# VectorE takes over the sums of squares and the sine products from GpSimd

## The chip, the cores and the metric

The kernel runs on one core of one Trainium2 chip, and all times are device microseconds (us) of that core. The core's engines run their own instruction streams and wait for each other through semaphores: TensorE (PE in the profile; PEld is its weight load), VectorE (DVE), ScalarE (ACT), GpSimd (POOL) and SyncE (SP), which starts the DMAs here.

## What is computed

Two networks run one after the other on 512 tokens of width 1024, all in float32. The first has two layers of this form:

```python
def hybrid_layer(x, ...):
    h = rms_norm(x, g_mix_pre)
    u = h @ w_in
    aq, ak, av, cu, rq, rk, rv, rg = jnp.split(u, SPLITS, axis=-1)
    y_att = chunk_attention(aq, ak, av, rel_bias)
    y_conv = conv_module(cu, conv_w, conv_b, conv_ln_g, conv_ln_b)
    y_ret = retention(rq, rk, rv, rg)
    mix = jnp.concatenate([y_att, y_conv, y_ret], axis=-1) @ w_out
    x = x + rms_norm(mix, g_mix_post)
    h = rms_norm(x, g_mlp_pre)
    f = jnp.square(jax.nn.relu(h @ w_up)) @ w_down
    return x + rms_norm(f, g_mlp_post)
```

`rms_norm` divides a row by the root of its mean square and multiplies by a gain. `retention` and one of the second network's attentions rotate queries and keys: `x1 * cos - x2 * sin`, `x2 * cos + x1 * sin`. The second network also has two layers, each a mixer of three attentions and a gated feed-forward (`silu(h @ w_gate) * (h @ w_up)) @ w_down`), with a plain residual after each.

## The kernel before

The activations stand with the 1024 features on partitions: eight tiles `x_1` to `x_8` (128 features by 512 tokens). Every product is made of three float32r matmuls. A weight chunk `raw` (128x1024) comes by DMA; ACT rounds it to `wh` (L511), DVE forms the rest `wl = raw - wh` (L513). A normalised input has `hh` from ACT (L682) and `hl` from DVE (L683). `dense` and `lin_tok` then issue `wh` by `hh`, `wh` by `hl` and `wl` by `hh` for each of the eight k (L529 to L531, and L546 to L548 in `lin_tok`), so one k needs all four.

A norm's factor is not applied to the input but to the product's output; it is made from a sum of squares over the features. `add_sq` squares a tile on ACT (`sq`, L677) and adds it to `acc` on POOL (L678). When all eight are in, PE sums over the partitions by a matmul with a column of ones (L663, into `po` or `pt`), DVE computes the inverse root in twelve small steps (`rstd`, L635 to L641) and spreads it (`bt`, L648), PE transposes that (L654) and ACT copies it to `rb` (L693), which every output of the product that follows is multiplied by.

Three places use it. `post_norm1` closes each half layer of the first network, in two halves of 256 tokens: after the half's factor, for each tile `f = f * gain * rb` (L1006), `x = x + f` (L1008), `hh`, `hl`, and the addition to `acc2`; of these additions the last tile's in the second half runs on DVE already (`DVE_ADDS = (7,)`), the others on POOL. `residual2` does the like in the second network for 512 tokens (L1025 for `x`), with one addition for each tile. The convolution's two channel halves are added once a layer (L887).

A rotation multiplies the tile by the cosine on DVE (L803), the tile with its halves swapped by DMA (`sw`) by the sine on POOL (L804, and L1400 in the second network), and adds the two on DVE (L805). L1386 multiplies the tables of cosine and sine by `rb` on POOL. POOL's other work is masks (L826, L1224) and memsets (L607, L1395).

The order of each engine's instructions is not the order of this code: the framework's scheduler replays the whole program with its own costs for each instruction and writes every engine's stream from that, so a change of an engine at some places moves rows on all engines. A weight's tile, `raw`, `wh` or `wl`, comes from a ring of buffers, and is reused when its last reader is done.

Of the kernel before, what the change touches and what calls it, by code (L numbers as in the profile page):

```python
# [15 lines left out]
ALU = mybir.AluOpType  # L16
# [45 lines left out]
HEAD_STEPS = 2  # L62
CHAIN = 2
FACTOR_LAG = 4
DVE_ADDS = (7,)

# [296 lines left out]
class Prog:  # L365
# [301 lines left out]
    def rms_bcast(self, accs, d, t0=0, t1=512, bank=None):  # L667
        return self.bcast_rows(self.mean_rstd(accs, d, t0, t1, bank), (t1 - t0) // 128, 1, bank)

    def add_sq(self, acc, x, first, eng=None):  # L670
        nc = self.nc
        if first:
            nc.scalar.activation(acc, x, AF.Square)
            return
        t = self.S(s="sq")
        w = t[:, :acc.shape[-1]]
        nc.scalar.activation(w, x, AF.Square)  # L677
        (eng or nc.gpsimd).tensor_tensor(acc, acc, w, op=ALU.add)  # L678

    def gained(self, x, g, hd, k, t0=0, t1=512):  # L680
        s, g = slice(t0, t1), g[:, k:k + 1]
# [100 lines left out]
    def mix1(self, l, hd, halves):  # L782
        nc, A = self.nc, self.A
# [10 lines left out]
        def rotated(nm, p):  # L794
            ps = opened.pop(nm) if p == 0 else self.lin(("w_in", nm, p), l, hd)
            j = 2 * (nm == "rk")
            raw, sw, ct, sn = self.scaled(ps, hd), self.S(s="sw"), self.S(s="ct"), self.S(s="sn")
            for a, b in ((0, 32), (32, 0), (64, 96), (96, 64)):
                nc.sync.dma_start(sw[a:a + 32], raw[b:b + 32])
            nc.sync.dma_start(ct, A["ret"][p, j])  # L800
            nc.sync.dma_start(sn, A["ret"][p, j + 1])
            yield
            nc.vector.tensor_tensor(raw, raw, ct, op=ALU.mult)  # L803
            nc.gpsimd.tensor_tensor(sw, sw, sn, op=ALU.mult)  # L804
            nc.vector.tensor_tensor(raw, raw, sw, op=ALU.add)  # L805
            if nm == "rq":
                rot["q", p] = self.movings(raw)
            else:
                rot["k", p] = [self.still(raw, i) for i in range(2)]
# [65 lines left out]
        def conv():  # L875
            cs = [self.S(s="cv") for _ in range(2)]
            for j in range(31):
                for p in range(2):
                    w, x = self.v("conv_w", l, 31 * p + j), cy[p][:, j:j + 512]
                    if j == 0:  # L880
                        nc.vector.tensor_scalar(cs[p], x, w, self.v("conv_b", l, p), op0=ALU.mult, op1=ALU.add)
                    else:
                        nc.vector.scalar_tensor_tensor(cs[p], x, w, cs[p], op0=ALU.mult, op1=ALU.add)
                if j % CONV_STEP == 0:
                    yield
            s = self.S(s="cs")
            nc.gpsimd.tensor_tensor(s, cs[0], cs[1], op=ALU.add)  # L887
            yield
            mu = self.ptr()
            mm(mu, self.m256, s, start=True, stop=True)  # L890
            acc = self.S(s="acc")
            for p in range(2):
                nc.vector.tensor_tensor(cs[p], cs[p], mu, op=ALU.subtract)
                self.add_sq(acc, cs[p], p == 0)
            yield
            rb = self.rms_bcast([acc], 256)
            z = []
            for p in range(2):
                z.append(self.S(s="z"))
                nc.vector.tensor_tensor(z[p], cs[p], rb, op=ALU.mult)  # L900
            yield
            for p in range(2):
                nc.scalar.activation(z[p], z[p], AF.Identity, scale=self.v("conv_ln_g", l, p),
                                     bias=self.v("conv_ln_b", l, p))
                t = self.S(s="th")
                nc.scalar.activation(t, z[p], AF.Tanh, scale=0.5)
                nc.vector.scalar_tensor_tensor(z[p], t, 1.0, z[p], op0=ALU.add, op1=ALU.mult)
            yield
            for p in range(2):
                mix[3 + p] = self.split(z[p], scale=0.5, s="mc")  # L910
# [36 lines left out]
        def out(o):  # L947
# [7 lines left out]
        opened = dict(zip(("rq", "rk"), self.open_mix((("w_in", "rv"), 384), [("w_in", "rq", 0), ("w_in", "rk", 0)],  # L955
                                                      l, hd, v_sink(rv), halves)))
        kinds = dict(rq=lambda p: rotated("rq", p), rk=lambda p: rotated("rk", p), cg=conv_gate, ca=conv_in,
                     ret=retention, conv=conv, rg=gate_ret, av=values, aq=att_q, ak=att_k, att=attention, wo=out)
        self.pipeline((job[0], kinds[job[0]](*job[1:])) for job in ORDER1)
        return mix, f  # L960
# [24 lines left out]
    def post_norm1(self, xs, f, g_post, g_next):  # L985

        nc = self.nc
        acc, last, acc2, hd = self.S(s="acc"), self.S(s="last"), self.S(s="acc2"), Normed(self)

        def sink(i, o, ps, t0, t1):  # L990
            s = slice(t0, t1)
            nc.vector.tensor_tensor(f[o][:, s], ps, f[o][:, s], op=ALU.add)
            if i < 7:
                self.add_sq(acc[:, s], f[o][:, s], i == 0)
            else:
                nc.scalar.activation(last[:, s], f[o][:, s], AF.Square)

        def done(t0, t1):
            s = slice(t0, t1)
            y = self.mean_rstd([acc, last], 1024, t0, t1)  # L1000
            yield
            yield
            rb = self.bcast_rows(y, (t1 - t0) // 128, 1)
            yield
            for o in range(8):
                nc.vector.scalar_tensor_tensor(f[o][:, s], f[o][:, s], g_post[:, o:o + 1], rb,  # L1006
                                               op0=ALU.mult, op1=ALU.mult)
                nc.vector.tensor_tensor(xs[o][:, s], xs[o][:, s], f[o][:, s], op=ALU.add)  # L1008
                self.gained(xs[o], g_next, hd, o, t0, t1)
                self.add_sq(acc2[:, s], xs[o][:, s], o == 0, nc.vector if t1 == 512 and o in DVE_ADDS else None)  # L1010
                if o % CHAIN == CHAIN - 1:
                    yield
            if t1 == 512:
                self.after = self.factor_parts(hd, [acc2], FACTOR_LAG)

        return sink, done, hd

    def residual2(self, xs, scale, g_next, final=False):
# [359 lines left out]
    def nsa_in(self, l, hd, nx, nm, p=None):  # L1378

        nc, A = self.nc, self.A  # L1380
        if not nx:
            nx["ct"], nx["sn"], nx["q"], nx["x"] = self.S(s="ct"), self.S(s="sn"), {}, {}
            nc.sync.dma_start(nx["ct"], A["rope"][0])
            nc.sync.dma_start(nx["sn"], A["rope"][1])
            for t in (nx["ct"], nx["sn"]):
                nc.gpsimd.tensor_tensor(t, t, hd.rb, op=ALU.mult)  # L1386
        ps = self.lin(("w_in_2", nm) + (() if p is None else (p,)), l, hd)
        if nm == "vc":
            raw = self.scaled(ps, hd)
            yield  # L1390
        else:
            raw = self.S(s="raw")
            self.copy("raw", raw, ps)
            sw = self.S(s="sw")
            nc.gpsimd.memset(sw, 0.0)  # L1395
            for a, b in ((0, 8), (8, 0), (64, 72), (72, 64)):
                nc.sync.dma_start(sw[a:a + 8], raw[b:b + 8])
            yield
            nc.vector.tensor_tensor(raw, raw, nx["ct"], op=ALU.mult)
            nc.gpsimd.tensor_tensor(sw, sw, nx["sn"], op=ALU.mult)  # L1400
            nc.vector.tensor_tensor(raw, raw, sw, op=ALU.add)
        if nm == "nq":
            for g in range(2):
                nx["q"][p, g] = self.still(raw, g, -0.125)
        elif nm in ("ks", "kw"):
            nx[nm == "kw"] = self.movings(raw)
        else:

            nat = self.split(raw, s="nat")
            o, _ = VEC["pos_" + nm[0], l]  # L1410
            pos = self.vec[:, o:o + 16]
            x = nx["x"][nm[0]] = self.pools["x"].tile([128, 2, 2, 512], F32R, tag="x", name=self.nm("xs"))
            for i in range(2):
                for g in range(2):
                    r = slice(64 * g, 64 * g + 64)
                    nc.sync.dma_start(x[0:64, i, g, 0:496].bitcast(F32), nat[i][r, 0:496].bitcast(F32))
                    nc.sync.dma_start(x[64:128, i, g, 0:496].bitcast(F32), nat[i][r, 16:512].bitcast(F32))
                    if i == 0:
                        self.hi(x[:, i, g, 496:512], pos)
                    else:  # L1420
                        self.lo(x[:, i, g, 496:512], pos, x[:, 0, g, 496:512])
# [191 lines left out]
```

## Time and profile before

| | us |
|---|---|
| time, median of 3 runs (lowest, highest) | 3353.74 (3351.65, 3353.86) |
| the profiled execution, its own time | 3348.55 |
| span of its trace, first to last instruction | 3346.80 |
| PE busy | 3261.0 (97%) |
| DVE busy | 1949.7 (58%), 3381 instructions |
| ACT busy | 1343.6 (40%) |
| POOL busy | 284.3 (8%), 341 instructions |
| mean granted TensorE clock | 0.992 of full speed |

The busy times are shares of the whole span, which has stages of quite different kinds: a mixer with small matmuls, softmaxes and rotations; a feed-forward of large matmuls; and short stretches between them in which the norm's chain on DVE must run before the next product can. TensorE's clock has two levels, 2.4 GHz (1.00 in the profile) and 1.2 GHz (0.50). 1.75 us of the execution's time lie outside the span.

### The profile page before, as it was taken

Reading aid. Unit: us, or ns where it says so; the run is one execution under the profiler, and the core shown is the slowest. Engines: PE = TensorE matmul, PEld = TensorE weight load, DVE = VectorE, ACT = ScalarE, POOL = GpSimd, SP = SyncE. Lnnn points to the kernel's source line nnn. Section 1 sums busy time; section 2 is a strip of 40 time slices with the busy share of each in tenths; the row PEclk is TensorE's granted clock in tenths of the full one; section 3 lists DMA queues with packets and bytes.
Section 4 is the critical chain, followed back from the end, with each engine's and each line's share of the span. In section 5 each row is a group of like instructions: output and inputs, shape, how many; then the busy total and the mean of one; then the engine's idle time right before and its main releaser. Section 6 shows DMA issues by size and latency. Waiting matters only on the chain. (4 is left out here: it accounts for less than half of the span.)

```text
span 3346.8 us, 41207 instructions
## 1 busy us (share of the span) xinstructions
PE 3261.0 (97%) x15956; PEld 2678.4 (80%) x15956; DVE 1949.7 (58%) x3381; ACT 1343.6 (40%) x2254; POOL 284.3 (8%) x341
## 2 busy tenths in 40 slices
PE   8999999899999999999999999999999999999998
PEld 7778888877888888888777678888888877778887
DVE  5977334789734456454678654545445478664454
ACT  4464323436533333222566722223222356642222
POOL 2111000221200020000210000001000120010001
PEclk9999999999999999999999999999999999999999
DMA  5212222332132222222323022222222323112222
GB/s 169 98 64 95 95 97 99 116 130 82 65 106 95 101 95 95 95 97 99 111 81 120 26 95 97 98 95 95 98 97 95 120 75 101 67 70 100 96 95 69
DMA packets 100868, 317.29 MB, mean 95 GB/s; under 512 B 12608, under 2 KB 18112, under 8 KB 100672
## 3 DMA queue, kind: packets, MB, share of 16 engines
q1 hardware_dynamic: 100672, 314.66, 27.5%
q8 instruction: 125, 2.05, 0.2%
q14 instruction: 71, 0.58, 0.1%
HBM read 298.75 MB, written 6.29 MB: 91 GB/s over the span
## 5 line engine op out<-in xcount | busy, mean ns | idle before, releaser
L511 ACT ACTIVATE wh<-raw 128x1024 fp32r<-128x1024 f32 (+2 forms) x546 | 567.5, 1041 | 1401.6 <-PE pd L530 582.4
L513 DVE TENSOR_TENSOR wl<-raw,wh 128x1024 fp32r<-128x1024 f32 (+2 forms) x546 | 666.3, 1222 | 435.3 <-ACT wh L511 433.7
L529 PE MATMUL pd<-hh,wh 128*128 128x512 f32 (+1 forms) x1328 | 508.8, 385 | 3.2 <-ACT wh L511 3.2
L530 PE MATMUL pd<-hl,wh 128*128 128x512 f32 (+1 forms) x1328 | 508.4, 383 | 3.6 <-DVE hl L683 3.1
L531 PE MATMUL pd<-hh,wl 128*128 128x512 f32 (+1 forms) x1328 | 507.1, 382 | 2.1 <-DVE wl L513 2.1
L678 POOL TENSOR_TENSOR acc<-acc,sq 128x256 f32<-128x256 f32 (+1 forms) x160 | 172.7, 1083 | 2151.0 <-ACT sq L677 2148.6
L529 PEld LDWEIGHTS pd<-hh,wh 128*128 128x128 f32 x1328 | 251.5, 190 | 51.8 <-issue 3.7
L530 PEld LDWEIGHTS pd<-hl,wh 128*128 128x128 f32 x1328 | 252.1, 190 | 50.8 <-DVE hl L683 5.4
L531 PEld LDWEIGHTS pd<-hh,wl 128*128 128x128 f32 x1328 | 252.0, 190 | 48.5 <-DVE wl L513 2.5
L530 PE MATMUL pt<-hl,wh 128*128 128x512 f32 x480 | 188.8, 394 | 8.2 <-DVE hl L683 8.2
L530 PE MATMUL ps<-hl,wh 128*128 128x512 f32 (+1 forms) x528 | 196.6, 372 | 0.0
L529 PE MATMUL ps<-hh,wh 128*128 128x512 f32 (+1 forms) x528 | 196.2, 372 | 0.0
L531 PE MATMUL ps<-hh,wl 128*128 128x512 f32 (+1 forms) x528 | 196.1, 372 | 0.0
L531 PE MATMUL pt<-hh,wl 128*128 128x512 f32 x480 | 188.2, 393 | 0.0
L529 PE MATMUL pt<-hh,wh 128*128 128x512 f32 x480 | 187.8, 393 | 0.0
L529 PE MATMUL pd<-ah,wh 128*128 128x512 f32 (+1 forms) x498 | 185.0, 372 | 0.0
L530 PE MATMUL pd<-al,wh 128*128 128x512 f32 (+1 forms) x498 | 184.8, 371 | 0.0
L531 PE MATMUL pd<-ah,wl 128*128 128x512 f32 (+1 forms) x498 | 184.8, 371 | 0.0
L587 ACT ACTIVATE ah<-sc 128x512 fp32r<-128x512 f32 x88 | 55.6, 632 | 184.0 <-DVE sc L1131 184.0
L529 PE MATMUL pt<-ah,wh 128*128 128x512 f32 (+1 forms) x332 | 123.5, 372 | 0.0
L530 PE MATMUL ps<-al,wh 128*128 128x512 f32 (+1 forms) x332 | 123.4, 372 | 0.0
L531 PE MATMUL ps<-ah,wl 128*128 128x512 f32 (+1 forms) x332 | 123.3, 371 | 0.0
(476 smaller groups left out, 6483.8 us busy)
## 6 DMA issues: line engine op xcount, KB each, us to landing
raw<-in_w SPq DMA_DIRECT2D x514, 512.0 KB
raw<-in_w SPq DMA_DIRECT2D x20, 384.0 KB
xd<-x SPq DMA_DIRECT2D x16, 256.0 KB
x<-xd SPq DMA_DIRECT2D x16, 256.0 KB
sw<-sc SPq DMA_DIRECT2D x48, 64.0 KB
ct<-in_ret SPq DMA_DIRECT2D x12, 256.0 KB
sn<-in_ret SPq DMA_DIRECT2D x12, 256.0 KB
mst<-in_bias SPq DMA_DIRECT2D x12, 256.0 KB
```

Source lines behind the costliest of these rows:

```text
L511: nc.scalar.activation(h[:, :n], raw[:, :n], AF.Copy)
L513: eng.tensor_tensor(lo[:, :n], raw[:, :n], h[:, :n].bitcast(F32), op=ALU.subtract)
L529: mm(ps, h, rh[j][:, t0:t1], start=first and j == 0, stop=False)
L530: mm(ps, h, rl[j][:, t0:t1], start=False, stop=False)
L531: mm(ps, lo, rh[j][:, t0:t1], start=False, stop=last and j == n - 1)
L587: self.nc.scalar.activation(dst, src, AF.Copy, scale=scale)
L678: (eng or nc.gpsimd).tensor_tensor(acc, acc, w, op=ALU.add)
```

## The change

Six places change. `add_sq` loses its argument for the engine, and its addition is always DVE's; the constant `DVE_ADDS` goes, so code lines behind it move up by one. The four other products and sums named above are DVE's as well.

```diff
-DVE_ADDS = (7,)
...
-    def add_sq(self, acc, x, first, eng=None):
+    def add_sq(self, acc, x, first):
...
-        (eng or nc.gpsimd).tensor_tensor(acc, acc, w, op=ALU.add)
+        nc.vector.tensor_tensor(acc, acc, w, op=ALU.add)
...
             nc.vector.tensor_tensor(raw, raw, ct, op=ALU.mult)
-            nc.gpsimd.tensor_tensor(sw, sw, sn, op=ALU.mult)
+            nc.vector.tensor_tensor(sw, sw, sn, op=ALU.mult)
...
-            nc.gpsimd.tensor_tensor(s, cs[0], cs[1], op=ALU.add)
+            nc.vector.tensor_tensor(s, cs[0], cs[1], op=ALU.add)
...
-                self.add_sq(acc2[:, s], xs[o][:, s], o == 0, nc.vector if t1 == 512 and o in DVE_ADDS else None)
+                self.add_sq(acc2[:, s], xs[o][:, s], o == 0)
...
             for t in (nx["ct"], nx["sn"]):
-                nc.gpsimd.tensor_tensor(t, t, hd.rb, op=ALU.mult)
+                nc.vector.tensor_tensor(t, t, hd.rb, op=ALU.mult)
...
             nc.vector.tensor_tensor(raw, raw, nx["ct"], op=ALU.mult)
-            nc.gpsimd.tensor_tensor(sw, sw, nx["sn"], op=ALU.mult)
+            nc.vector.tensor_tensor(sw, sw, nx["sn"], op=ALU.mult)
```

190 instructions leave POOL: 114 additions of 128x256 and 46 of 128x512 (L678), 24 sine products (L804, L1400), 4 products of tables (L1386), 2 sums of the convolution (L887).

The scheduler's new order is shown at three places; in these rows a tile's name ends in a running number, `x_125` is the eighth tile of the activations, and the column at the end is partitions by elements.

The first place is DVE between the first network's first feed-forward and its second mixer (634 to 650 us of the trace). Before, in the middle of the chain of the second half's last tiles:

```order
L1006 SCALAR_TENSOR_TENSOR f_3488<-f_3488,vec,pt_5388 128x256
L683 SCALAR_TENSOR_TENSOR hl_4885<-x_124,vec,hh_4877 128x256
L1008 TENSOR_TENSOR x_125<-x_125,f_3488 128x256
L513 TENSOR_TENSOR wl_5490<-raw_5487,wh_5489 128x768
L683 SCALAR_TENSOR_TENSOR hl_4886<-x_125,vec,hh_4878 128x256
L678 TENSOR_TENSOR acc_852_4870<-acc_852_4870,sq_5478 128x256
L513 TENSOR_TENSOR wl_5520<-raw_5517,wh_5519 128x768
L513 TENSOR_TENSOR wl_5552<-raw_5549,wh_5551 128x768
```

The changed kernel has the same two conversions, `wl_5490` and `wl_5520`, in front of the chain, which begins with `f_3209`:

```order
L512 TENSOR_TENSOR wl_5458<-raw_5455,wh_5457 128x1024
L639 SCALAR_TENSOR_TENSOR a_5355<-a_5355,v_5353 128x2
L512 TENSOR_TENSOR wl_5490<-raw_5487,wh_5489 128x768
L640 SCALAR_TENSOR_TENSOR y_5354<-a_5355,y_5354 128x2
L647 COPY bt_5386<-y_5354 128x256
L512 TENSOR_TENSOR wl_5520<-raw_5517,wh_5519 128x768
L1005 SCALAR_TENSOR_TENSOR f_3209<-f_3209,vec,pt_5388 128x256
```

Both conversions have moved from the end of a chain of some 32 instructions to its start.

The second place is DVE between the second network's first mixer and its feed-forward (1922 to 1932 us). Before:

```order
L1025 SCALAR_TENSOR_TENSOR x_15167<-ps_16274,x_15167 128x512
L683 SCALAR_TENSOR_TENSOR hl_16114<-x_15163,vec,hh_16106 128x512
L513 TENSOR_TENSOR wl_16334<-raw_16331,wh_16333 128x1024
L513 TENSOR_TENSOR wl_16365<-raw_16362,wh_16364 128x1024
L683 SCALAR_TENSOR_TENSOR hl_16115<-x_15165,vec,hh_16107 128x512
L683 SCALAR_TENSOR_TENSOR hl_16116<-x_15167,vec,hh_16108 128x512
L635 TENSOR_SCALAR v_16298<-po_16293 128x4
```

The changed kernel, from the same `hl_16114` on:

```order
L682 SCALAR_TENSOR_TENSOR hl_16114<-x_15163,vec,hh_16106 128x512
L512 TENSOR_TENSOR wl_16253<-raw_16250,wh_16252 128x1024
L677 TENSOR_TENSOR acc_16100<-acc_16100,sq_16246 128x512
L1024 SCALAR_TENSOR_TENSOR x_15165<-ps_16249,x_15165 128x512
L1024 SCALAR_TENSOR_TENSOR x_15167<-ps_16274,x_15167 128x512
L512 TENSOR_TENSOR wl_16334<-raw_16331,wh_16333 128x1024
L682 SCALAR_TENSOR_TENSOR hl_16115<-x_15165,vec,hh_16107 128x512
L677 TENSOR_TENSOR acc_16100<-acc_16100,sq_16271 128x512
L682 SCALAR_TENSOR_TENSOR hl_16116<-x_15167,vec,hh_16108 128x512
L677 TENSOR_TENSOR acc_16100<-acc_16100,sq_16290 128x512
L512 TENSOR_TENSOR wl_16365<-raw_16362,wh_16364 128x1024
```

One of the two conversions that stood ahead of `hl_16115` and `hl_16116` now stands behind them; another, `wl_16253`, has come in from further ahead.

The third place is PE in the first network's first feed-forward (283 to 286 us), around the sum over the partitions of `acc2` (`po_2845`), whose second pair of matmuls waits for the second half's last addition. Before, that pair stands among the sixth tile's matmuls (`hh_2196`):

```order
L529 MATMUL ps_2584<-hh_2196,wh_2588 128x256
L530 MATMUL ps_2584<-hl_2204,wh_2588 128x256
L663 MATMUL po_2845<-ones_89,acc_421_2190 128x1 x2
L531 MATMUL ps_2584<-hh_2196,wl_2589 128x256
L529 MATMUL ps_2585<-hh_2196,wh_2638 128x256
```

The changed kernel has it between the seventh tile's (`hh_2197`) and the last one's (`hh_2198`):

```order
L529 MATMUL ps_2585<-hl_2205,wh_2638 128x256
L530 MATMUL ps_2585<-hh_2197,wl_2639 128x256
L662 MATMUL po_2845<-ones_89,acc_421_2190 128x1 x2
L528 MATMUL pd_2582<-hh_2198,wh_2290 128x256
L529 MATMUL pd_2582<-hl_2206,wh_2290 128x256
```

Sixteen matmuls of 128x256 have come in front of the pair.

## Rows read from the trace of the kernel before

**Rows 1.** The page: busy us (share of the span) and instructions of each engine.

```profile
PE 3261.0 (97%) x15956; PEld 2678.4 (80%) x15956; DVE 1949.7 (58%) x3381; ACT 1343.6 (40%) x2254; POOL 284.3 (8%) x341
```

**Rows 2.** Waits of PE: line, waited for whom; us in total, times, longest us.

```profile
PE pt L530 <- DVE hl L683: 8.2, 2, 4.1
PE ps L548 <- DVE wl L513: 7.9, 4, 6.8
...
PE po L663 <- DVE acc L678: 5.0, 3, 1.7
```

**Rows 3.** Lines of POOL by shape: names, shapes, count | busy us, mean ns | idle before.

```profile
L678 POOL TENSOR_TENSOR acc<-acc,sq 128x256 f32<-128x256 f32 x114 | 98.8, 871 | 853.6 <-ACT sq L677 852.1
L678 POOL TENSOR_TENSOR acc<-acc,sq 128x512 f32<-128x512 f32 x46 | 73.9, 1607 | 1297.4 <-ACT sq L677 1296.5
...
L804 POOL TENSOR_TENSOR sw<-sw,sn 128x512 f32<-128x512 f32 x12 | 17.3, 1441 | 91.7 <-DMA sn<-in_ret 64.1 <-DVE wl L513 26.6 <-PE pd L531 1.0
```

**Rows 4.** Lines of DVE by shape, the same columns.

```profile
L513 DVE TENSOR_TENSOR wl<-raw,wh 128x1024 fp32r<-128x1024 f32 x514 | 639.0, 1244 | 430.6 <-ACT wh L511 429.4
...
L683 DVE SCALAR_TENSOR_TENSOR hl<-x,vec,hh 128x512 fp32r<-128x512 f32 x48 | 46.6, 977 | 18.1 <-ACT hh L682 18.1
L1008 DVE TENSOR_TENSOR x<-x,f 128x256 f32<-128x256 f32 x64 | 41.3, 662 | 0.0
L683 DVE SCALAR_TENSOR_TENSOR hl<-x,vec,hh 128x256 fp32r<-128x256 f32 x64 | 38.1, 595 | 1.8 <-ACT hh L682 1.7
...
L805 DVE TENSOR_TENSOR sc<-sc,sw 128x512 f32<-128x512 f32 x12 | 8.2, 684 | 3.8 <-POOL sw L804 3.5
```

**Rows 5.** Timeline of DVE, 634 to 650 us: start us, duration us, instruction [idle before].

```profile
634.70 1.22 DVE L513 TENSOR_TENSOR wl<-raw,wh 128x1024 fp32r<-128x1024 f32 x1
...
638.08 0.42 DVE L1008 TENSOR_TENSOR x<-x,f 128x256 f32<-128x256 f32 x1
638.42 0.48 DVE L683 SCALAR_TENSOR_TENSOR hl<-x,vec,hh 128x256 fp32r<-128x256 f32 x1
638.81 0.48 DVE L1006 SCALAR_TENSOR_TENSOR f<-f,vec,pt 128x256 f32<-128x256 f32 x1
...
646.95 0.94 DVE L513 TENSOR_TENSOR wl<-raw,wh 128x768 fp32r<-128x768 f32 x1
...
648.22 0.41 DVE L678 TENSOR_TENSOR acc<-acc,sq 128x256 f32<-128x256 f32 x1
```

**Rows 6.** Timeline of PE, 640 to 658 us.

```profile
647.95 0.69 PE L548 MATMUL ps<-wl,hh 128*128 128x384 f32 x1 [6.77 <-DVE wl L513]
...
657.70 0.28 PE L529 MATMUL pd<-hh,wh 128*128 128x256 f32 x1
```

**Rows 7.** Timeline of ACT, 648 to 652 us.

```profile
650.84 0.84 ACT L511 ACTIVATE wh<-raw 128x768 fp32r<-128x768 f32 x1 [2.96 <-DMA raw<-in_w]
```

**Rows 8.** Timeline of DVE, 1924 to 1934 us.

```profile
1925.24 4.52 DVE L513 TENSOR_TENSOR wl<-raw,wh 128x1024 fp32r<-128x1024 f32 x2
1929.68 2.41 DVE L683 SCALAR_TENSOR_TENSOR hl<-x,vec,hh 128x512 fp32r<-128x512 f32 x2
```

**Rows 9.** Timeline of PE, 1926 to 1936 us.

```profile
1931.48 0.79 PE L530 MATMUL pt<-hl,wh 128*128 128x512 f32 x1 [4.12 <-DVE hl L683]
```

**Rows 10.** Timeline of PE, 282 to 290 us.

```profile
285.27 0.61 PE L663 MATMUL po<-ones,acc 128*128 128x1 f32 x4 [1.66 <-DVE acc L678]
```

**Rows 11.** Stretches A:B: us, busy of PE, PEld, DVE, ACT, POOL; granted clock, DMA share, GB/s.

```profile
120.00:140.00 20.00, 20.00 (x116) 19.02 (x115) 19.86 (x33) 9.79 (x15) 3.13 (x6) 1.00 0.38 132
284.00:292.00 8.00, 6.73 (x39) 6.32 (x40) 4.55 (x18) 3.04 (x5) 0.00 (x0) 0.79 0.00 0
644.00:652.00 8.00, 4.05 (x14) 4.05 (x15) 6.65 (x11) 2.73 (x6) 1.93 (x3) 0.57 0.31 108
1928.00:1936.00 8.00, 4.52 (x17) 3.80 (x18) 4.36 (x5) 1.06 (x1) 2.80 (x2) 0.79 0.39 131
2968.00:2980.00 12.00, 8.94 (x26) 7.39 (x27) 7.18 (x18) 1.06 (x1) 2.38 (x2) 0.57 0.31 112
```

## The prediction

> **What bounds the kernel now.** I read the page first: PE is busy for 3261.0 of 3346.80 us, so the kernel runs at the pace of its matmuls, and DVE and POOL matter only where PE waits for them or loses its clock after such a wait [rows 1]. The waits of PE come second. Three lines stand out that hang on what the change touches: the lower half `hl` of a normalised tile, 8.2 us in two waits; the weight's rest `wl`, 7.9 us, nearly all in one; and the last addition to a sum of squares, 5.0 us in three [rows 2]. Then I read those places in the timelines and the clock of the stretches around them. Everything else in the change is judged by whether it lengthens or shortens these waits or makes new ones.
>
> **What the moved work costs on DVE.** POOL loses 98.8 + 73.9 us for 160 additions and 17.3 us for 12 of the 30 products and sums [rows 3]; with the other 18 at the same 1.44 us that is 216 us, and POOL falls from 284 to about 68. On DVE an addition of 128x256 lasts 0.41 us, and its like, L1008, is followed by the next instruction after 0.34 us [rows 5]; a 128x512 addition lasts 0.68 us (L805) [rows 4]. So DVE gains 114 x 0.34 + 76 x 0.68 = 91 us.
>
> **What DVE gets back.** DVE's instructions that read two SBUF tiles are longer than their shortest in this trace. L1008 takes 0.42 us in the clear [rows 5] and 0.662 in the mean [rows 4]: 64 x 0.24 = 15 us. `hl` of 128x256 takes 0.48 us against 0.595, 64 x 0.115 = 7 us; `hl` of 128x512 0.977 against 0.684 of its like L805, 48 x 0.29 = 14 us [rows 4, 5]. `wl` takes 1.22 us in the clear and 2.26 each beside POOL's additions [rows 5, 8]; over 514 of them the mean is 1.244, 12 us [rows 4]. I put this to POOL's additions, beside which the long ones stand. That is 48 us back, and DVE ends near 1950 + 91 - 48 = 1993 us; between no relief and twice this relief, 1945 to 2041. For the span only the places count.
>
> **Place one, 634 to 658 us (first order piece).** PE idles 6.77 us for `wl` [rows 6], since that conversion stands at the end of DVE's chain (at 646.95) [rows 5], and the clock is at 0.57 in the mean of 644 to 652 [rows 11]. In the new order two conversions go first. The chain then starts about 2 x 0.9 us later, at 637.6, and takes 8 f, 8 x, 8 `hl` and 7 additions: 16 x 0.39 + 15 x 0.34 = 11.3 us, and 0.9 for one conversion that stays inside [rows 5]. It ends at 649.8. PE follows it tile by tile, because the weights are there, and has six matmuls left after the last `hl`: about 651.5 to 652.5 for what stood at 657.70 [rows 6]. That saves 5.5 us. What could take it back stands on ACT: two weights are rounded in front of the third and the fourth tile's `hh` there, and a `wh` of this stretch waited 2.96 us for its DMA, which itself had waited for a `raw` buffer [rows 7]. The conversions that free those buffers also come earlier, so I allow for 2 us of delay at most, which would leave 3.5.
>
> **Place two, 1922 to 1936, and its twin in the second layer (second order piece).** PE idles 4.12 us for `hl` [rows 9]; the two conversions ahead of it took 4.52 us, the two `hl` 2.41 [rows 8]. Then the clock falls: 0.79 over 8 us costs 1.7 us, and in the twin 0.57 over 12 us costs 5.2, of which one lies in the idle time [rows 11]. In the new order one conversion (1.2 us instead of 2.3) and two additions (1.3 us) stand in the way, and PE has some seven matmuls of the next product, 1.6 us, ahead of the one that waits. I expect `hl` 2 us earlier and a wait of about 0.4 us, too short to cost the clock. Saved: 4.1 + 1.7 - 0.4 = 5.4, and in the twin 4.1 + 4.2 - 0.4 = 7.9; together 13.
>
> **Place three, the sums in the three second halves (third order piece).** 1.66 us for DVE's last addition [rows 10], 5.0 us in three waits [rows 2], and at the one shown 0.79 over 8 us, another 1.7 [rows 11]. Sixteen matmuls of 0.12 us come in front, 1.9 us, and the chain ahead of the addition has no net growth (7 x 0.34 more, four to five stretched instructions x 0.54 less). Saved: about 6 of 6.7. Some conversions now stand inside the inverse root there; they make `rb` some 3 us later, which the next product's 24 large matmuls hide; without that cover it would cost those 3 us each.
>
> **The rest.** Rotations: the sine product ran beside the cosine product and took 1.44 us; on DVE both take 1.4 in a row, so the chain is level. The first halves of the norms: additions and relief level within 1 us each. Of these and of the mixers' new order the trace shows no price; the bounds are a saving of 10 (the remaining waits for norms) and a cost of 26 (below), and I take a cost of 2, since PE's short waits there are mostly on ACT. Sum: -5.5 - 13 - 6 + 2 = -22.5. From the profiled execution's 3348.55 that is 3326; the median of the runs stands 5.2 us above it, and 3353.7 - 22.5 gives **3331**. The measurement tells changes from about 0.2%, 6.7 us.
>
> **Rivals.** *DVE becomes late.* In the first network's mixers DVE is already full, 19.86 of 20 us [rows 11], and in the norms' chains every instruction follows the last. If the long instructions are not POOL's doing, there is no relief: each of the six norm halves gets 8 x 0.34 = 2.7 us longer, 16 us, and PE, which follows these chains, waits for it and drops its clock, 1.7 us each time, 10 us more. Of the savings, those at place two and one shrink to half. 26 - 12 is 14 slower: 3368. It decides if L1008 stays above 0.55 us. For it speaks the full DVE; against it that the short and the long forms differ by 0.54 us beside POOL's additions and that POOL has none left. The Trainium skill (Perfetto Trace Analysis, section Optimizing Scalar/DVE Operations) speaks for this rival where it says that work may go from a saturated DVE even to GpSimd; the same passage warns that the two share a read port, so that this might not help, and the stretched rows here agree with the warning.
>
> *Given back.* The savings are made, but the new order makes waits of its own elsewhere (a conversion or a rounding that waits for its DMA with a chain behind it on the same engine, as in [rows 7]); seven waits of 3 us would do. 3350.
>
> *More is gained.* The first halves and the mixers lose their short waits as well, another 10 us: 3321.
>
> **How the numbers follow.** Forecast 0.55, more gained 0.14, given back 0.16, late 0.15. Faster 0.69, same 0.16, slower 0.15. The forecast's own range is 3322 to 3344 (place one without 2 us, place two half, against the bound of 10). The range for 8 in 10 takes in the case of a gain given back and leaves out most of the late one: 3317 to 3356.
>
> **What would show it.** In the changed profile: POOL near 68 us; L1008 near 0.42 us and `hl` of 128x512 near 0.7; DVE between 1945 and 2041. PE's waits for `wl` in `lin_tok` and for `hl` should be under 2 us each in total, and the clock's dips near 648, 1934 and 2974 gone. The forecast is wrong if L1008 stays long, or if PE's waits show new lines of several us, on `rb`'s transposes or on `wh` from DMA.

## The result and the profile after

The changed kernel takes 3306.65 us (median of 4 runs, 3302.28 to 3308.04) against 3353.80 for the kernel before on the same chip: a ratio of 0.9864, with a 95% interval from 0.9852 to 0.9876. It is 47 us faster, twice the 22.5 that were forecast, and below the range, which ended at 3317. The mechanism was the forecast one. What went wrong was mostly one term of the sum, the rest beside the three named places. One execution among the ten of the run of products and sums below (13871 us, at a granted clock of 0.22) is left out of its ratio.

The page of the changed kernel, its span and the busy time of each engine, which answers to [rows 1]:

```profile
span 3303.7 us, 40955 instructions
...
PE 3251.5 (98%) x15956; PEld 2673.1 (81%) x15956; DVE 1964.7 (59%) x3571; ACT 1345.8 (41%) x2254; POOL 70.0 (2%) x151
```

The span is 43.1 us shorter. 9.5 us of that are PE's busy time (3261.0 to 3251.5), for the same matmuls. Most of it is the clock, which stood at 0.50 for some 44 us of the trace before and for 27 us now, program start and end left out. The other 33.6 are PE's idle time. DVE has 190 instructions more and only 15 us more busy time.

DVE's lines by shape (names, shapes, count | busy us, mean ns | idle before), which answer to [rows 3, 4], say why:

```profile
L512 DVE TENSOR_TENSOR wl<-raw,wh 128x1024 fp32r<-128x1024 f32 x514 | 628.5, 1223 | 415.9 <-ACT wh L510 414.8 <-DMA xs<-nath 0.3
...
L677 DVE TENSOR_TENSOR acc<-acc,sq 128x256 f32<-128x256 f32 x118 | 48.8, 421 | 11.9 <-ACT sq L676 11.2
L682 DVE SCALAR_TENSOR_TENSOR hl<-x,vec,hh 128x512 fp32r<-128x512 f32 x48 | 35.9, 748 | 17.0 <-ACT hh L681 17.0
L677 DVE TENSOR_TENSOR acc<-acc,sq 128x512 f32<-128x512 f32 x46 | 31.5, 686 | 0.0
L682 DVE SCALAR_TENSOR_TENSOR hl<-x,vec,hh 128x256 fp32r<-128x256 f32 x64 | 30.7, 480 | 1.7 <-ACT hh L681 1.4
...
L1007 DVE TENSOR_TENSOR x<-x,f 128x256 f32<-128x256 f32 x64 | 25.7, 419 | 0.0
```

`x` is at 0.419 us where it had 0.662, `hl` at 0.480 and 0.748 where it had 0.595 and 0.977, `wl` at 1.223 where it had 1.244. The moved additions last 0.42 and 0.69 us, and lasted 0.87 and 1.61 on POOL.

Where the long forms came from shows in the kernel before, in the chain at place one. POOL's line holds two additions, which ended at 639.50 and 640.38:

```profile
638.68 1.69 POOL L678 TENSOR_TENSOR acc<-acc,sq 128x256 f32<-128x256 f32 x2 [7.22 <-ACT sq L677]
```

```profile
638.81 0.48 DVE L1006 SCALAR_TENSOR_TENSOR f<-f,vec,pt 128x256 f32<-128x256 f32 x1
639.20 0.57 DVE L683 SCALAR_TENSOR_TENSOR hl<-x,vec,hh 128x256 fp32r<-128x256 f32 x1
639.70 0.96 DVE L1008 TENSOR_TENSOR x<-x,f 128x256 f32<-128x256 f32 x1
```

`hl` and `x` read two SBUF tiles each, and each ended 0.28 us after the addition beside which it had started. So it is in the whole trace: 30 of the 64 `x` started while one of POOL's additions ran, and every one ended 0.28 to 0.29 us after it; the other 34 took 0.41 to 0.42 us. `f` reads one SBUF tile and `pt`, which lies in PSUM; all 20 that started beside an addition took their usual 0.47 to 0.48.

PE's waits (line, waited for whom: us in total, times, longest) answer to [rows 2]:

```profile
PE ps L545 <- ACT wh L510: 6.9, 1, 6.9
PE ps L547 <- DVE wl L512: 5.6, 2, 2.8
...
PE pd L530 <- DVE wl L512: 3.1, 1, 3.1
...
PE pt L662 <- DVE acc L677: 1.9, 1, 1.9
```

The wait of 8.2 us for `hl` is gone, that for `wl` in `lin_tok` is down from one of 6.8 to two of 2.8 (5.6 in all, where the prediction named under 2 as its sign), a wait for `wl` in the last norm of the first network is up from 1.5 to 3.1, and `po` waits no longer for the last addition (1.9 us are left at the very end of the program, into `pt`).

The table shows by how much the same matmuls start earlier than before, as the two timelines give it, once the stretch is over. Each layer of the second network has a feed-forward on either side of its mixer.

| up to, in the trace of before | us earlier | what the stretch holds |
|---|---|---|
| 115 us | 6.0 | first mixer, first half |
| 240 | 6.3 | its second half |
| 290 | 7.2 | norm, both halves (place three) |
| 660 | 11.9 | place one |
| 860 | 13.3 | second mixer |
| 900 | 12.7 | norm (place three) |
| 1270 | 16.6 | second feed-forward, norm (place three) |
| 1620 | 19.5 | the second network's first feed-forward, its end |
| 1900 | 22.2 | its first mixer |
| 1950 | 28.0 | place two |
| 2660 | 30.4 | two feed-forwards, their ends (0.9 and 1.5) |
| 2950 | 34.3 | its second mixer |
| 2990 | 42.2 | place two's twin |
| 3346 | 43.1 | rest |

Place two went as the prediction describes it. DVE's timeline there:

```profile
1904.45 1.22 DVE L512 TENSOR_TENSOR wl<-raw,wh 128x1024 fp32r<-128x1024 f32 x1
1905.59 0.75 DVE L682 SCALAR_TENSOR_TENSOR hl<-x,vec,hh 128x512 fp32r<-128x512 f32 x1
1906.25 0.69 DVE L677 TENSOR_TENSOR acc<-acc,sq 128x512 f32<-128x512 f32 x1
1906.85 0.75 DVE L682 SCALAR_TENSOR_TENSOR hl<-x,vec,hh 128x512 fp32r<-128x512 f32 x1
1907.51 0.69 DVE L677 TENSOR_TENSOR acc<-acc,sq 128x512 f32<-128x512 f32 x1
1908.11 1.22 DVE L512 TENSOR_TENSOR wl<-raw,wh 128x1024 fp32r<-128x1024 f32 x1
```

Before, the same stretch was two conversions in 4.52 us and two `hl` in 2.41 [rows 8]; now one conversion, two `hl` and two additions take 3.7. The stretches that answer to [rows 11] (us, busy of PE, PEld, DVE, ACT, POOL; granted clock, DMA share, GB/s) show the clock:

```profile
276.00:284.00 8.00, 7.78 (x62) 7.19 (x60) 6.63 (x21) 4.51 (x9) 0.00 (x0) 1.00 0.01 2
...
634.00:642.00 8.00, 6.07 (x30) 4.64 (x28) 7.72 (x22) 5.47 (x13) 1.04 (x2) 1.00 0.13 53
1900.00:1908.00 8.00, 8.00 (x37) 6.63 (x36) 8.00 (x12) 4.41 (x7) 0.00 (x0) 1.00 0.32 113
2930.00:2942.00 12.00, 12.00 (x58) 10.02 (x57) 10.88 (x24) 4.50 (x6) 0.00 (x0) 1.00 0.50 175
```

All four are at 1.00, where the answering ones had 0.79, 0.57, 0.79 and 0.57. But the first halves of two norms lost their clock. After:

```profile
258.00:268.00 10.00, 9.05 (x50) 8.59 (x51) 7.66 (x25) 1.94 (x5) 0.00 (x0) 0.66 0.32 107
868.00:884.00 16.00, 14.92 (x81) 13.89 (x80) 11.96 (x38) 3.73 (x10) 0.00 (x0) 0.68 0.20 67
```

and before:

```profile
264.00:274.00 10.00, 8.72 (x64) 7.88 (x65) 9.02 (x24) 1.62 (x5) 2.53 (x4) 1.00 0.33 107
880.00:896.00 16.00, 13.97 (x96) 12.95 (x95) 14.43 (x36) 6.04 (x17) 6.44 (x8) 0.89 0.19 67
```

### The profile page after: what moved, and what is told of

Read it like the earlier page. It is cut to its first block, busy times and chain, and to the rows that moved or that the text cites. A ratio compares the mean times of both kernels' runs of the same rounds, so it can differ in the third digit from the quotient of the medians.

```text
span 3303.7 us, 40955 instructions
## 1 busy us (share of the span) xinstructions
PE 3251.5 (98%) x15956; PEld 2673.1 (81%) x15956; DVE 1964.7 (59%) x3571; ACT 1345.8 (41%) x2254; POOL 70.0 (2%) x151
## 4 chain that ended last, share of the span: by engine, by line
PE 90%; DVE 5%; ACT 2%; DMA 1%; issue 1%; SPq 0%; DVEq 0%; ACTq 0%
PE pd L528 12%; PE pd L529 12%; PE pd L530 12%; PE ps L530 6%; PE ps L528 6%; PE ps L529 6%; PE pt L528 6%; PE pt L529 6%; PE pt L530 6%; PE po L528 3%; PE po L530 3%; PE po L529 3%; PE po L777 3%; PE pt L745 2%; DVE wl L512 1%; PE ps L617 1%
## 5 line engine op out<-in xcount | busy, mean ns | idle before, releaser
L512 DVE TENSOR_TENSOR wl<-raw,wh 128x1024 fp32r<-128x1024 f32 (+2 forms) x546 | 654.4, 1200 | 420.0 <-ACT wh L510 418.8
L530 PE MATMUL pt<-ah,wl 128*128 128x512 f32 (+1 forms) x332 | 123.2, 371 | 0.0
```

What stands on the lines that cost most here:

```text
L512: eng.tensor_tensor(lo[:, :n], raw[:, :n], h[:, :n].bitcast(F32), op=ALU.subtract)
L530: mm(ps, lo, rh[j][:, t0:t1], start=False, stop=last and j == n - 1)
```

## Experiments

Every kernel is given as a ratio to the kernel before on its chip, with its 95% interval; the microseconds beside it are that ratio's difference from 1 by 3351.

**The two parts apart.** The theory (A in the expectations) was that GpSimd's instructions on SBUF hold up VectorE's that read two SBUF tiles, so that each part of the change gains where its own instructions stood beside a chain. The rival (B) was that the scheduler's new order gains, whatever is moved. First the additions alone:

```diff
-        (eng or nc.gpsimd).tensor_tensor(acc, acc, w, op=ALU.add)
+        nc.vector.tensor_tensor(acc, acc, w, op=ALU.add)
```

> Only the 160 additions of squares are VectorE's; the 30 sine products, table products and convolution sums stay on GpSimd. Theory A (VectorE's instructions on two SBUF tiles are held up by GpSimd's, so whoever leaves GpSimd frees the chain beside it): the places where only additions were beside the chain keep their gains, 5 at 634 to 660 us, 13 at the two places after the second network's mixers, some 5 in the norms' halves, some 6 more at the other ends; the mixers' 13 are missing. 3321, L1008 at 0.42 us. Theory B (the scheduler's new order is what gains, and any change of engines reshuffles it): the time has no relation to which part was moved; anything from 3300 to 3350, and the mixers' stretches, where nothing was moved, change by several us as well.

Measured: 3320.3 us, 0.9911 (0.9896 to 0.9926), 30 us faster. Then the 30 products and sums alone:

```diff
-            nc.gpsimd.tensor_tensor(sw, sw, sn, op=ALU.mult)
+            nc.vector.tensor_tensor(sw, sw, sn, op=ALU.mult)
...
-            nc.gpsimd.tensor_tensor(s, cs[0], cs[1], op=ALU.add)
+            nc.vector.tensor_tensor(s, cs[0], cs[1], op=ALU.add)
...
-                nc.gpsimd.tensor_tensor(t, t, hd.rb, op=ALU.mult)
+                nc.vector.tensor_tensor(t, t, hd.rb, op=ALU.mult)
...
-            nc.gpsimd.tensor_tensor(sw, sw, nx["sn"], op=ALU.mult)
+            nc.vector.tensor_tensor(sw, sw, nx["sn"], op=ALU.mult)
```

> Only the sine products, the table products and the convolution's sum are VectorE's; the additions of squares stay on GpSimd. Theory A: what the mixers gained, 6 in the first 110 us, 1 in the first network's second mixer, 3 and 4 in the second network's mixers, some 13 in all: 3341, L1008 stays at 0.66 us. Theory B: a time without relation to that, and the stretches after the mixers change too.

Measured: 3342.81 us, 0.9970 (0.9961 to 0.9980), 10 us faster. `x` is at 0.416 us in the first run and at 0.662 in the second, as theory A has it. The parts make 40 of the whole's 46 (0.9864); the 6 left lie within the intervals of the three ratios (4 to 5 us each way for the two large ones).

The traces tell where each part gains. The table gives us gained against the kernel before, one execution of each:

| | four mixers | all other stretches |
|---|---|---|
| whole change | 14.4 | 28.7 |
| additions alone | -0.5 | 29.5 |
| products and sums alone | 12.8 | -7.8 |

Each part gains where its own instructions stood, and the additions alone give all that the change gives outside the mixers. The loss of 7.8 us, where the second run moved nothing, is spread over many stretches, none over 2.6 us; it tells how much a new order and the difference between executions can do here.

**The additions by size.** Only those of 128x512, most of them at the ends of the second network's mixers and feed-forwards:

```diff
-        (eng or nc.gpsimd).tensor_tensor(acc, acc, w, op=ALU.add)
+        (eng or (nc.vector if acc.shape[-1] == 512 else nc.gpsimd)).tensor_tensor(acc, acc, w, op=ALU.add)
```

> Only the 46 additions of 128x512 are VectorE's, the 114 of 128x256 and the sine products stay on GpSimd. Theory A: the two places after the second network's mixers give their 13.5 and the ends of its feed-forwards some 3: 3337, hl of 128x512 at 0.75 us while L1008 stays at 0.66. Theory B: those places need not gain.

Measured: 3334.57 us, 0.9952 (0.9935 to 0.9969), 16 us faster. Of DVE's lines, the two that matter:

```profile
L1008 DVE TENSOR_TENSOR x<-x,f 128x256 f32<-128x256 f32 x64 | 41.3, 662 | 0.0
...
L683 DVE SCALAR_TENSOR_TENSOR hl<-x,vec,hh 128x512 fp32r<-128x512 f32 x48 | 35.8, 746 | 15.9 <-ACT hh L682 15.9
```

And only those of 128x256, with `== 256` in that line:

> Only the 114 additions of 128x256 in the first network are VectorE's; those of 128x512 and the sine products stay on GpSimd. If the parts add up, the additions' 31 us less the 17 of the 128x512 ones, 14 us: 3337, L1008 at 0.42 us, hl of 128x512 at 0.98. By the prediction's places one and three, 11.5: 3340. If the order decides, no relation to that.

Measured: 3337.57 us, 0.9963 (0.9949 to 0.9977), 12 us faster. DVE's same two lines there:

```profile
L683 DVE SCALAR_TENSOR_TENSOR hl<-x,vec,hh 128x512 fp32r<-128x512 f32 x48 | 50.7, 1064 | 18.6 <-ACT hh L682 18.6
...
L1008 DVE TENSOR_TENSOR x<-x,f 128x256 f32<-128x256 f32 x64 | 25.7, 421 | 0.0
```

Each size of addition frees the lines that stand beside it and leaves the others long, and 16 + 12 is the 30 of both within the error. That is A's picture; B gives no reason for it.

**GpSimd's load back, without its results.** The changed kernel, and GpSimd adds each tile of squares to itself into a tile that nobody reads:

```diff
         nc.vector.tensor_tensor(acc, acc, w, op=ALU.add)
+        nc.gpsimd.tensor_tensor(self.shd[:, :acc.shape[-1]], w, w, op=ALU.add)
```

> The changed kernel, and beside each of its additions GpSimd adds the same squares to themselves into a tile that nobody reads: GpSimd has the load of before, but no chain waits for it. Theory A: L1007 goes back to about 0.6 us, and the chains are longer by it; of the gain about half or more is lost again, 3325 to 3345. Theory C (the additions' own time on GpSimd, 0.87 and 1.6 us against 0.42 and 0.69, was what the chains lost): nothing waits for GpSimd, so the gain stays, 3306 to 3312. Theory B: the order changes little, the gain stays as well.

Measured: 3364.76 us, 1.0041 (1.0026 to 1.0056), 59 us slower than the changed kernel and slower than the kernel before. Theory C falls for the additions: nothing waits for these results, and all of the gain goes. Theory A had the direction and missed both numbers: the loss is larger than its 3325 to 3345, and `x` is at 0.466 us and not at 0.6, since now other instructions stand beside GpSimd's: `hl` (0.618 and 0.924 us) and the additions (0.546 and 1.271). Theory B falls here altogether: in this trace PE's 15956, ACT's 2254 and DVE's 3571 instructions run in the same order, one by one (by line, tile name and shape), as in the changed kernel's, and 59 us are lost with no change of order. Nor does the longer hold of the squares' buffer cost anything that shows: no square on ACT waits for GpSimd in this trace. DVE's timeline beside two of GpSimd's additions, at place two's end:

```profile
1938.66 1.21 DVE L513 TENSOR_TENSOR wl<-raw,wh 128x1024 fp32r<-128x1024 f32 x1
1939.79 1.52 DVE L684 SCALAR_TENSOR_TENSOR hl<-x,vec,hh 128x512 fp32r<-128x512 f32 x1
1941.24 1.52 DVE L678 TENSOR_TENSOR acc<-acc,sq 128x512 f32<-128x512 f32 x1
1942.68 0.74 DVE L684 SCALAR_TENSOR_TENSOR hl<-x,vec,hh 128x512 fp32r<-128x512 f32 x1
1943.35 0.68 DVE L678 TENSOR_TENSOR acc<-acc,sq 128x512 f32<-128x512 f32 x1
```

and POOL's:

```profile
1939.55 2.66 POOL L679 TENSOR_TENSOR shd<-sq 128x512 f32<-128x512 f32 x2 [4.97 <-ACT sq L677]
```

`hl` and the addition take 1.52 us each while POOL works, and 0.74 and 0.68 as soon as it is done.

**The same GpSimd instructions, writing only.** In place of that addition GpSimd clears the squares' tile, which it can do only when VectorE is done with it:

```diff
         nc.vector.tensor_tensor(acc, acc, w, op=ALU.add)
+        nc.gpsimd.memset(w, 0.0)
```

> The changed kernel, and behind each addition GpSimd clears the tile of squares that was just added: as many GpSimd instructions in the same places as in the shadow run, holding the same buffer a little longer, but they only write. If GpSimd's reading of SBUF is what holds VectorE up, VectorE's instructions keep their short times (additions 0.42 and 0.69, hl of 128x512 0.75) and the time stays within 3303 to 3315. If instead the longer hold of the buffer, the scheduler's order or any GpSimd work makes the shadow run slow, this one is slow as well, 3335 to 3365.

Measured: 3311.01 us, 0.9883 (0.9868 to 0.9897), 6 us slower than the changed kernel with an error of about as much, and within the 3303 to 3315 that stood for the reading. DVE's additions and POOL's new lines:

```profile
L677 DVE TENSOR_TENSOR acc<-acc,sq 128x256 f32<-128x256 f32 x118 | 48.7, 420 | 11.8 <-ACT sq L676 11.2
...
L677 DVE TENSOR_TENSOR acc<-acc,sq 128x512 f32<-128x512 f32 x46 | 31.5, 684 | 0.0
```

```profile
L678 POOL MEMSET sq<- 128x256 f32 x118 | 36.8, 312 | 914.5 <-DVE acc L677 900.8 <-DVE y L635 5.4 <-PE pt L530 3.1
...
L678 POOL MEMSET sq<- 128x512 f32 x46 | 24.2, 527 | 1386.3 <-DVE acc L677 1118.5 <-PE pd L530 188.0 <-DVE st L721 74.9
```

164 GpSimd instructions that hold the buffer stretch nothing and cost little, and the order of PE, ACT and DVE is again the changed kernel's, one by one. They are shorter than the additions (0.31 and 0.53 against 0.79 and 1.40 us; 61 us in all against 157). That does not explain the difference: VectorE's busy time rose by 1.5 us here (1964.7 to 1966.2) and by 64.3 in the shadow run, and the 14 `x` that started beside one of these memsets took 0.41 to 0.42 us. With the run before it, GpSimd's reading is what the loss hangs on.

**VectorE's load alone.** The changed kernel with the useless additions on VectorE:

```diff
         nc.vector.tensor_tensor(acc, acc, w, op=ALU.add)
+        nc.vector.tensor_tensor(self.shd[:, :acc.shape[-1]], w, w, op=ALU.add)
```

> The changed kernel, and behind each addition VectorE adds the same squares to themselves into a tile that nobody reads: 118 x 0.42 + 46 x 0.69, some 65 us (by starts) to 81 us more on VectorE and nothing on GpSimd. It has about the extra VectorE time of the shadow additions (64 us) without GpSimd beside them. Theory D (what counts is VectorE's time in the chains, whatever it is spent on): as slow as the shadow additions, 3350 to 3370. Theory A in its narrow form (GpSimd beside VectorE does more harm than its stretching shows): 3315 to 3330.

Measured: 3338.16 us, 0.9961 (0.9947 to 0.9976), 32 us slower than the changed kernel; both theories missed it. VectorE's busy time rose by 61.5 us (1964.7 to 2026.2), in the shadow run by 64.3 (to 2029.0), and the two cost 32 and 59 us. A microsecond of its own work in these places cost about half a microsecond, one of being held up by GpSimd nearly a whole one. The two are not quite alike: the scheduler planned for the additions on VectorE, and 651 of DVE's 3571 shared instructions and 1354 of PE's 15956 stand elsewhere than in the changed kernel, while the shadow run kept its order. Whether that is why the second is dearer was not settled.

**The rotations' two halves.** The sine products alone (L804 and L1400), and the four products of the tables alone (L1386), in the kernel before:

> The kernel before with only the 24 sine products on VectorE. If their chains were level, as the prediction took it, 3351 as before. If they carry most of what the rotations' run gained (8.7 us): 3345.

> The kernel before with only the four products of the rotation's tables on VectorE: on GpSimd two in a row took 3.5 us ahead of the second network's first rotation, on VectorE 1.4. If the rotation waits for them, 2 us at each of two places: 3347. If not: 3351.

Measured: 3345.58 us, 0.9987 (0.9977 to 0.9996), 4 us faster, and 3348.03 us, 0.9990 (0.9981 to 0.9999), 3 us faster. Each differs from no change by little more than its error (1 to 8 us and 0 to 6); with the run of both, 10 us (6.7 to 13), both seem to count.

**The masks too.** The last readers on GpSimd, 80 triangular masks, were made products with a tile of zeros and ones on VectorE:

```diff
-                nc.gpsimd.affine_select(pt[kt][:, 0:128], pt[kt][:, 0:128], pattern=[[1, 128]],
-                                        compare_op=ALU.is_ge, fill=0.0, base=0, channel_multiplier=-1)
+                nc.vector.tensor_tensor(pt[kt][:, 0:128], pt[kt][:, 0:128], self.upper, op=ALU.mult)
```

and likewise for the other mask.

> The changed kernel, and the 80 triangular masks of 128x128 go to VectorE as well, as products with a constant tile of zeros and ones (0.25 to 0.3 us each in place of 0.35 and 0.60 on GpSimd, some 21 us more on VectorE); GpSimd then reads nothing in the layers. If the remaining reads still hold VectorE up, or the masks' way over GpSimd is on a chain, 3 to 6 us faster than the changed kernel, 3301; if VectorE's load in the full mixers costs as in the doubled additions (32 us for 81), 5 to 8 slower, 3313.

Measured: 3308.32 us, 0.9877 (0.9863 to 0.9892), not to be told from the changed kernel. What the masks free and what they cost on VectorE cancel, or both are nothing. There was little to free: the 19 taps of the convolution that started beside a mask in the changed kernel took 0.74 to 0.78 us, against a median of 0.74 over all 120.

## Why the prediction fell short

*The moved work and what VectorE gets back*: right. POOL was put near 68 us and has 70.0. The relief was put at 48 us; the four lines give 15.6 for `x`, 7.4 and 10.7 for `hl`, 10.5 for `wl`, 44 together. DVE was put near 1993 and has 1964.7: if the moved work is the 91 us it was counted at, by starts, the whole relief was 76, and 32 of it lie in lines that the prediction left out, such as the cosine products (0.876 to 0.696 us, 2 us) and the convolution's taps (0.763 to 0.745, 2 us).

*Place one*: 5.5 forecast, 4.7 measured over both halves of its norm (7.2 to 11.9 in the table). The new order did what the prediction read from it, with one thing missed: for the conversion that stays inside the chain it had counted DVE's 0.9 us, and not that PE waits for it. PE's and DVE's rows:

```profile
643.14 0.45 PE L547 MATMUL ps<-wl,hh 128*128 128x384 f32 x1 [2.79 <-DVE wl L512]
```

```profile
631.89 0.87 DVE L1005 SCALAR_TENSOR_TENSOR f<-f,vec,pt 128x256 f32<-128x256 f32 x2
...
642.13 0.95 DVE L512 TENSOR_TENSOR wl<-raw,wh 128x768 fp32r<-128x768 f32 x1
...
644.13 0.42 DVE L677 TENSOR_TENSOR acc<-acc,sq 128x256 f32<-128x256 f32 x1
```

The chain takes 12.7 us from its first `f` to its last addition, 12.2 in the prediction; but PE waits 2.8 us in it for that weight. The other wait of 2.8 us for `wl` is in the first half of the same norm (617.02) and new as well; the sum had no term for it.

*Place two*: 13.3 forecast, 5.8 + 7.9 = 13.7 measured.

*Place three*: 6 forecast for the second halves, with the first halves level. Over both halves of the three norms the table gives 0.9, -0.6 and 3.9, 4.2 together. The waits of 1.66 us are gone. The first halves were not level: in two of them PE now waits up to 0.93 us for `hh`, and the clock falls behind that to a mean of 0.66 over 10 us and 0.68 over 16, where it had 1.00 and 0.89. By the clock alone that is 3.4 us lost in the one and 3.4 in the other, an estimate from these rows.

*The rest* is the step that failed. It was priced at a cost of 2 us, and gained about 20: 6.3 in the first mixer, 1.4 in the second, 2.7 and 3.9 in the second network's, 2.9 at the end of its first feed-forward, 0.9 and 1.5 at the ends of the next two, 0.9 at the end of the program. Of the 6.3 the first 1.5 lie ahead of the first rotation, and the run of the tables, which changes nothing there, shows 1.2 as well, so they may be chance.

For the mixers the sentence that did it says that the rotations' chain is level, since the sine product "ran beside the cosine product and took 1.44 us". The two did not run beside each other. They are two products of two SBUF tiles each, on POOL and DVE, and one waited for the other. In the kernel before, the first rotation, POOL and DVE:

```profile
51.53 1.83 POOL L804 TENSOR_TENSOR sw<-sw,sn 128x512 f32<-128x512 f32 x1 [14.52 <-DMA sn<-in_ret]
```

```profile
51.54 0.68 DVE L803 TENSOR_TENSOR sc<-sc,ct 128x512 f32<-128x512 f32 x1
53.40 0.69 DVE L805 TENSOR_TENSOR sc<-sc,sw 128x512 f32<-128x512 f32 x1 [1.18 <-POOL sw L804]
```

and the second:

```profile
58.98 1.40 POOL L804 TENSOR_TENSOR sw<-sw,sn 128x512 f32<-128x512 f32 x1 [5.03 <-DMA sn<-in_ret]
```

```profile
59.13 1.79 DVE L803 TENSOR_TENSOR sc<-sc,ct 128x512 f32<-128x512 f32 x1
61.03 0.69 DVE L805 TENSOR_TENSOR sc<-sc,sw 128x512 f32<-128x512 f32 x1
```

The second one in the changed kernel, on DVE alone:

```profile
57.81 0.68 DVE L802 TENSOR_TENSOR sc<-sc,ct 128x512 f32<-128x512 f32 x1
58.41 0.69 DVE L803 TENSOR_TENSOR sw<-sw,sn 128x512 f32<-128x512 f32 x1
59.13 0.69 DVE L804 TENSOR_TENSOR sc<-sc,sw 128x512 f32<-128x512 f32 x1
```

In the first rotation the cosine product took its usual 0.68 us and the sine product 1.83, where the shortest in the trace is 1.28. In the second the cosine product was held until POOL was done at 60.38 and ended 0.54 us later. From the first product's start to the sum's end they took 2.6 and 2.7 us, and take 2.0 both; the prediction's 1.44 + 0.69 would have been 2.1. Not every rotation is like these: of the 24 cosine products four were held (1.28 to 1.80 us), and many a sine product was over before its cosine product began. How much of the mixers' gain is the turns that the two engines took, and how much the sine products' own length on POOL (1.28 to 2.10 us against 0.7), the runs do not separate. The waits for the matmuls that follow the rotations (L618) went: of 3.6 us that PE waited in the first mixer between 60 and 240 us, 2.1 of them there, 0.4 are left and none there. The prediction had the mechanism, it had priced it for `x`, `hl` and `wl`, and it did not apply it to the products that stood side by side in the same lines of code. The warning stood in its rows, too: L805 had waited 3.5 us for POOL [rows 4]. The rotations' run measures this term, with the tables and the convolution's sum: 10 us where 0 was put.

The additions were forecast at 24.5 by the places and measured at 30: 16 for the large ones, which beside place two's 13 gain at the feed-forwards' ends, 12 for the small ones. With the 2 us of cost that did not come, 10 + 5.5 + 2 are 17.5 of the 24 us by which the forecast was short. The other 6 are the difference between the whole and its parts, within the error of the runs. That the three places came out near their 24.5 in sum (22.6) is in part luck, since the losses in the first halves, which the forecast had not seen, were made up by larger gains in the second (at place one the lead went from 7.2 to about 5 and then to 11.9 us).

*The rivals.* "DVE becomes late" was priced at 3368 for the case that VectorE gets no relief. Its condition was not met, since L1007 fell to 0.42, so its price stays untested: the shadow run took 3365, but there the long instructions are POOL's doing. Its 12 us of savings left do not come out of its own words either; half of 13 and 5.5 is 9, and the upper end of the forecast's own range, 3344, is 4 above what its words give. "Given back" happened in part, in the first halves of the norms: the waits of 2.8 and 3.1 us for `wl` there and the two clock rows above show it, and the gains outweighed it. "More is gained" is what came, and it was held too small, at 10 us beyond the forecast, because it was thought of as a few short waits and not as the main mechanism in four more stages.

## What to carry to other kernels

When GpSimd and VectorE share the elementwise work of one chain, look for VectorE instructions of one shape with two lengths, and see what GpSimd does beside the long ones: here the work went from 214 us on GpSimd to some 100 on VectorE, and VectorE's busy time grew by 15. Price such a conflict in every pair of instructions that the code puts side by side, not only where TensorE's largest waits stand; the other stages, of which the trace showed no large wait, were about half of the gain. A useless instruction on the suspected engine, with nothing waiting for it, shows the conflict by itself, and one that only writes shows whether it is the reading. Compare the order of the other engines' instructions in such runs: here it had stayed the same, one by one, which rules the scheduler out.

## What the hardware showed

- A VectorE instruction on two SBUF tiles that starts during a GpSimd addition or product mostly ends a fixed time after that one: the 30 `x` of 128x256 all 0.28 to 0.29 us after it (0.42 us long by themselves), a cosine product of 128x512 at 60.92, 0.54 us after GpSimd's end at 60.38 (0.68 by itself). In the kernel before, 95 of 97 such `x`, `hl`, `wl` and cosine products were held, and the other two had started within 0.02 us of GpSimd's start and went first; in the shadow run 123 of 138 were. `f`, with one of its tiles in PSUM, is not held (20 of 20 at 0.47 to 0.48 us). The Trainium skill (SBUF — State Buffer, section Who interferes with whom) has this as an exclusive lock held for a whole instruction, and the trace agrees; it also says there that a GpSimd instruction that only writes does not contend with such a VectorE instruction, and the run with memsets agrees (0.420 and 0.684 us beside them, 0.421 and 0.686 without).
- 61.5 us more of VectorE's own work beside the sums of squares cost 32 us of time (with an order of its own), and 64.3 us more of being held up cost 59 (in the same order), in a kernel in which TensorE is busy for 98% of the span.
